# Cross attention from split halves, both token tiles in one values product, and seven weight buffers instead of nine

## The chip, the core and the metric

The kernel runs on one core of a Trainium2 chip. The core has five engines with a queue each: TensorE (PE in the profile, with its weight loads as PEld), VectorE (DVE), ScalarE (ACT), GpSimd (POOL) and SyncE (SP), which here issues the weight transfers. The metric is the device time of one execution in microseconds.

## What is computed

Two transformer blocks run over one sequence of 256 tokens with a model width of 1024. The first has four layers. Each layer is a mixer (sliding-window attention, a gated linear recurrence, latent attention, sliding-window attention again), then a cross attention over 256 memory tokens, then a convolutional gated feed-forward part with a hidden width of 2816; each of the three ends in a residual sum and a layer norm. The second block has a dilated attention beside a retention, an MLP and a per-layer embedding part. The change is in the cross attention and in what is shared by all:

```python
def memory_cross_attention(x, mem_k, mem_v, w_q, w_o):
    q = (x @ w_q).reshape(bsz, s, X_HEADS, X_HEAD_DIM)          # 4 heads of 256
    sc = jnp.einsum('bshd,bmhd->bhsm', q, mem_k) * (X_HEAD_DIM ** -0.5)
    p = jax.nn.softmax(sc, axis=-1)
    o = jnp.einsum('bhsm,bmhd->bshd', p, mem_v).reshape(bsz, s, D_MODEL)
    return o @ w_o

mem_k, mem_v = jnp.split(mem @ mem_w_kv, 2, axis=-1)            # once, for all four layers
```

All inputs and outputs are float32.

## The kernel before

The 256 tokens are two tiles of 128 (t = 0, 1). Most products are made of halves: `split` (L204 to L206) makes a high part with a ScalarE copy that rounds to the type fp32r, and a low part with a VectorE subtraction of it. A product is then three fp32r matmuls, high x high, high x low, low x high (`mm_nat` L219 to L221, weights as the moving side; `mm_T` L227 to L229, weights as the stationary side).

Weights stream from HBM. A tile is 128 x 1024 numbers, loaded by SP into one of five raw buffers and split in two halves of 512 columns into a `wh` and a `wl` buffer, of which there are nine each (L388, `self.wp`). ScalarE's copy into a buffer can start when TensorE has run the last matmul on the tile that had the buffer before, and VectorE's subtraction follows the copy. A projection of both token tiles with a width of 1024 goes over eight tiles: those of the first pass (t = 0) are used again in the pass over t = 1, so eight tiles are wanted at a time. Output projections do this in `out_steps` (L348 to L358), whose first token tile has the PSUM banks `acc, acc` and whose second has `po, tq`.

The order of instructions on each engine is not the order of the code: a scheduler places each instruction when it estimates that its inputs and a free buffer are there. So the number of buffers has a part in the order of all engines. At run time each engine runs its instructions in the placed order, one after another.

Names in the profile: `b0` to `b3` are the layers of the first block; `swa`, `lru`, `mla` the mixers, `mo` a mixer's output projection, `x` the cross attention, `xo` its output projection, `f` the feed-forward part. `dp0` is the first projection of the second block.

Cross attention (L457 to L524): the query of one token tile and half of the heads (`n`) is projected, copied to SBUF (L467), transposed by TensorE into the bank `tq` and copied by VectorE (L470); the scores are sixteen float32 matmuls of 256 columns (L480) per layer; the softmax follows (L483 to L492), the turn of the probabilities (transposes, one ScalarE copy L499), and the values as thirty-two float32 matmuls of 128 columns (L508), for one token tile and half at a time, from K and V of the memory that `memkv` made in the first mixer (L446, L453). A helper, `Skew`, issues the four units in a staggered order.

In the recurrent mixer of layer 1 (`b1lru`) the last gate needs TensorE's last matmul of the input projection, a `tanh` on ScalarE (L914, with a table load ahead of it) and a scan on VectorE (L904), and only then comes the last operand of the output projection `b1mo` (L924).

Of the kernel before, what the change touches and what calls it, by code (L numbers as in the profile page):

```python
# [19 lines left out]
P = 128  # L20
# [56 lines left out]
def col(n):  # L77
    return slice(n * 512, n * 512 + 512)


def tok(t):
    return slice(t * P, (t + 1) * P)
# [86 lines left out]
class Net:  # L169
# [117 lines left out]
    def T_split(self, src, hi, lo, n=4):  # L287
        self.split(self.transp(src, n), hi, lo)

    def rsqrt(self, v, n, eps):  # L290
# [136 lines left out]
    def memkv(self, mp):  # L427
# [3 lines left out]
        for t in range(NT):  # L431
# [6 lines left out]
        self.memk = self.memp.tile([P, KD, T], F32, name="memk")  # L438
        self.memv = self.memp.tile([P, 2, D], F32, name="memv")
# [17 lines left out]
    def cross(self, i):  # L457
# [3 lines left out]
        sc = 256.0 ** -0.5  # L461

        def query(t, n):
# [4 lines left out]
            pt = self.transp(q, 4, "tq")  # L468
            qT = self.s("q", [4, P])
            nc.vector.tensor_copy(qT, pt)  # L470
            return qT

        def attn(t, n, qT):
            p = self.s("p", [2, T])

            def scores():
                pss = self.ps("sc", (2, T))
                for h in range(2):
                    for k in range(2):
                        nc.tensor.matmul(pss[:, h], qT[:, 2 * h + k], self.memk[:, 4 * n + 2 * h + k],  # L480
                                         start=k == 0, stop=k == 1)
                nm = self.tiny("nm", [2])
                nc.vector.tensor_reduce(nm, pss, AX, ALU.max)  # L483
                nc.vector.tensor_scalar_mul(nm, nm, -sc)
                sm = self.tiny("den", [2])
                for h in range(2):
                    nc.scalar.activation(p[:, h], pss[:, h], AF.Exp, bias=nm[:, h : h + 1], scale=sc,
                                         accum_out=sm[:, h : h + 1])
                rs = self.tiny("rd", [2])
                nc.vector.reciprocal(rs, sm)  # L490
                for h in range(2):
                    nc.vector.tensor_scalar_mul(p[:, h], p[:, h], rs[:, h : h + 1])  # L492

            pTs = []

            def turn():
                pTs.append(self.s("pT", [2, 2, P]))
                pt = self.transp(p.rearrange("p a n -> p (a n)"))
                nc.scalar.activation(pTs[0].rearrange("p a b n -> p (a b) n"), pt, AF.Copy)  # L499

            def values():
                pT = pTs[0]
                po = self.ps("po", (4, P))
                for h in range(2):
                    for dt in range(2):
                        for m in range(2):
                            c = (2 * n + h) * 256 + dt * P
                            nc.tensor.matmul(po[:, 2 * h + dt], self.memv[:, m, c : c + P], pT[:, h, m],  # L508
                                             start=m == 0, stop=m == 1)
                sl = (slice(None), slice(4 * n, 4 * n + 4), tok(t))  # L510
                self.split(po, oTh[sl], oTl[sl])

            return scores, turn, values

        sk = Skew()
        todo = [(t, n) for t in range(NT) for n in range(2)]
        qs = [query(*todo[0])]
        for x, tn in enumerate(todo):
            if x + 1 < len(todo):
                qs.append(query(*todo[x + 1]))  # L520
            sk.unit(*attn(*tn, qs[x]))
        sk.flush()
        self.phase += "o"
        self.out_proj(self.cols(I["x_w_o"][i], 0, D), oTh, oTl, self.ln_tail(i, 1))  # L524


    def ffn_cols(self, i):
# [535 lines left out]
    def block1(self):  # L1063
        I = self.I
        n = 0
        with ExitStack() as c2:
# [9 lines left out]
            for i in range(DEPTH):  # L1076
# [18 lines left out]
                    return True  # L1095
                self.phase = f"b{i}x"
                cc = self.ffn_cols(i)
                self.cross(i)
                n += 1
                if n == self.stop:  # L1100
                    return True
# [588 lines left out]
```

## Time and profile before

| | us |
|---|---|
| median of 3 runs (2049.38 to 2052.22) | 2050.79 |
| the profiled execution | 2047.92 |
| its span | 2046.1 |
| TensorE busy | 2018.9 (99%), 10759 records |
| VectorE busy | 1586.5 (78%) |
| ScalarE busy | 1244.9 (61%) |
| HBM read over the span | 175 GB/s |

The profile is of one execution. The granted clock of TensorE is a share of full speed (1.0 is 2.4 GHz, 0.5 is 1.2 GHz). A float32 matmul leaves two records, an fp32r matmul one. The duration of a matmul in a row is longer than its place in the queue, since matmuls overlap: what one costs is read from the distance between the starts of neighbours.

### The profile page before, as it was taken

Reading aid. Unit: us, or ns where it says so; the run is one execution under the profiler, and the core shown is the slowest. Engines: PE = TensorE matmul, PEld = TensorE weight load, DVE = VectorE, ACT = ScalarE, POOL = GpSimd, SP = SyncE. Lnnn points to the kernel's source line nnn. Section 1 sums busy time; section 2 is a strip of 40 time slices with the busy share of each in tenths; the row PEclk is TensorE's granted clock in tenths of the full one; section 3 lists DMA queues with packets and bytes.
Section 4 is the critical chain, followed back from the end, with each engine's and each line's share of the span. In section 5 each row is a group of like instructions: output and inputs, shape, how many; then the busy total and the mean of one; then the engine's idle time right before and its main releaser. Section 6 shows DMA issues by size and latency. Waiting matters only on the chain.

```text
span 2046.1 us, 30433 instructions
## 1 busy us (share of the span) xinstructions
PE 2018.9 (99%) x10759; PEld 1701.3 (83%) x10759; DVE 1586.5 (78%) x3146; ACT 1244.9 (61%) x2592; POOL 40.2 (2%) x55
## 2 busy tenths in 40 slices
PE   9999999999999999999999999999999999999998
PEld 7878888887888888888887788888998888788887
DVE  7766898899699887679888778988677666676666
ACT  6745766595477646457766557665676444556554
POOL 0000000000000000000000000000000000000000
PEclk9999999999999999999999999999999999999999
DMA  8463666447457544565654445764545555566662
GB/s 265 136 193 118 204 215 196 150 132 240 141 179 227 173 150 144 176 205 165 207 166 154 146 135 198 227 192 118 170 150 191 163 181 191 165 205 206 192 192 76
DMA packets 236809, 359.65 MB, mean 176 GB/s; under 512 B 13936, under 2 KB 157424, under 8 KB 236656
## 3 DMA queue, kind: packets, MB, share of 16 engines
q1 hardware_dynamic: 236656, 357.71, 54.8%
q8 instruction: 84, 1.38, 0.3%
q14 instruction: 69, 0.57, 0.1%
HBM read 356.60 MB, written 1.05 MB: 175 GB/s over the span
## 4 chain that ended last, share of the span: by engine, by line
PE 51%; DVE 4%; ACT 2%; issue 1%; DMA 1%; POOL 0%; SPq 0%; DVEq 0%; POOLq 0%; ACTq 0%
PE b2f.sc L253 2%; PE b2f.tr L253 2%; PE b3f.sc L253 1%; PE b3f.tr L253 1%; PE mlp.sc L253 1%; PE mlp.tr L253 1%; PE mlp.acc L219 1%; PE mlp.acc L221 1%; PE mlp.acc L220 1%; PE b3f.acc L219 1%; PE b3f.acc L220 1%; PE b3f.acc L221 1%; PE b2f.acc L221 1%; PE b2f.sc L257 1%; PE b2f.acc L219 1%; PE b2f.acc L220 1%
## 5 line engine op out<-in xcount | busy, mean ns | idle before, releaser
L206 DVE TENSOR_TENSOR mlp.wl<-mlp.raw,mlp.wh 128x512 fp32r<-128x512 f32 x132 | 86.1, 687 | 41.2 <-ACT mlp.wh L205 40.1
L205 ACT ACTIVATE mlp.wh<-mlp.raw 128x512 fp32r<-128x512 f32 x132 | 75.7, 624 | 37.8 <-PE mlp.tq L221 20.8
L205 ACT ACTIVATE b1f.wh<-b1f.raw 128x512 fp32r<-128x512 f32 x132 | 76.3, 623 | 30.0 <-PE b1xo.tq L221 11.0
L205 ACT ACTIVATE b2f.wh<-b2f.raw 128x512 fp32r<-128x512 f32 x132 | 76.1, 622 | 28.9 <-PE b2xo.tq L221 11.0
L205 ACT ACTIVATE b0f.wh<-b0f.raw 128x512 fp32r<-128x512 f32 x132 | 76.2, 622 | 27.9 <-PE b0xo.tq L221 11.0
L205 ACT ACTIVATE b3f.wh<-b3f.raw 128x512 fp32r<-128x512 f32 x132 | 76.4, 622 | 26.7 <-PE b3xo.tq L221 9.8
L206 DVE TENSOR_TENSOR b2f.wl<-b2f.raw,b2f.wh 128x512 fp32r<-128x512 f32 x132 | 85.6, 683 | 4.6 <-ACT b2f.wh L205 4.3
L206 DVE TENSOR_TENSOR b0f.wl<-b0f.raw,b0f.wh 128x512 fp32r<-128x512 f32 x132 | 85.5, 683 | 4.7 <-ACT b0f.wh L205 4.5
L206 DVE TENSOR_TENSOR b1f.wl<-b1f.raw,b1f.wh 128x512 fp32r<-128x512 f32 x132 | 85.4, 683 | 4.7 <-ACT b1f.wh L205 4.5
L206 DVE TENSOR_TENSOR b3f.wl<-b3f.raw,b3f.wh 128x512 fp32r<-128x512 f32 x132 | 85.7, 684 | 4.3 <-ACT b3f.wh L205 4.1
L253 PE MATMUL b3f.sc<-b3xo.xT,b3f.wh 128*128 128x512 f32 x144 | 52.4, 398 | 1.0 <-DVE b3f.e L563 1.0
L253 PE MATMUL b1f.sc<-b1xo.xT,b1f.wh 128*128 128x512 f32 x144 | 52.4, 398 | 0.0
L253 PE MATMUL b0f.sc<-b0xo.xT,b0f.wh 128*128 128x512 f32 x144 | 52.4, 398 | 0.0
L253 PE MATMUL b2f.sc<-b2xo.xT,b2f.wh 128*128 128x512 f32 x144 | 52.3, 397 | 0.0
L253 PE MATMUL b0f.tr<-b0xo.xT,b0f.wh 128*128 128x512 f32 x144 | 51.7, 394 | 0.0
L253 PE MATMUL b1f.tr<-b1xo.xT,b1f.wh 128*128 128x512 f32 x144 | 51.7, 394 | 0.0
L253 PE MATMUL b3f.tr<-b3xo.xT,b3f.wh 128*128 128x512 f32 x144 | 51.7, 394 | 0.0
L253 PE MATMUL b2f.tr<-b2xo.xT,b2f.wh 128*128 128x512 f32 x144 | 51.7, 394 | 0.0
L563 DVE SCALAR_TENSOR_TENSOR b0f.e<-b0f.p,b0x.cols,b0f.e 128x255 f32<-128x255 f32 (+1 forms) x72 | 34.2, 479 | 7.0 <-ACT b0f.e L561 6.6
L563 DVE SCALAR_TENSOR_TENSOR b2f.e<-b2f.p,b2x.cols,b2f.e 128x255 f32<-128x255 f32 (+1 forms) x72 | 34.2, 479 | 6.6 <-ACT b2f.e L561 6.1
L563 DVE SCALAR_TENSOR_TENSOR b1f.e<-b1f.p,b1x.cols,b1f.e 128x255 f32<-128x255 f32 (+1 forms) x72 | 34.2, 478 | 6.5 <-ACT b1f.e L561 6.0
L563 DVE SCALAR_TENSOR_TENSOR b3f.e<-b3f.p,b3x.cols,b3f.e 128x255 f32<-128x255 f32 (+1 forms) x72 | 34.2, 479 | 5.6 <-ACT b3f.e L561 5.1
(1651 smaller groups left out, 7073.2 us busy)
## 6 DMA issues: line engine op xcount, KB each, us to landing
b0f.raw<-in_f_w_up_dram SPq DMA_DIRECT2D x44, 512.0 KB
b1f.raw<-in_f_w_up_dram SPq DMA_DIRECT2D x44, 512.0 KB
b2f.raw<-in_f_w_up_dram SPq DMA_DIRECT2D x44, 512.0 KB
b3f.raw<-in_f_w_up_dram SPq DMA_DIRECT2D x44, 512.0 KB
mlp.raw<-in_w_up_dram SPq DMA_DIRECT2D x32, 512.0 KB
mlp.raw<-in_w_down_dram SPq DMA_DIRECT2D x32, 512.0 KB
b0f.raw<-in_f_w_down_dram SPq DMA_DIRECT2D x22, 512.0 KB
b1f.raw<-in_f_w_down_dram SPq DMA_DIRECT2D x22, 512.0 KB
```

What stands on the lines that cost most here:

```text
L205: self.nc.scalar.activation(hi, src, AF.Copy)
L206: self.nc.vector.tensor_sub(lo, src, hi.bitcast(F32))
L219: mm(ps, Th[:, k, tok(t)], wh, start=start, stop=False)
L220: mm(ps, Th[:, k, tok(t)], wl, start=False, stop=False)
L221: mm(ps, Tl[:, k, tok(t)], wh, start=False, stop=stop)
L253: mm(ps.rearrange("p a n -> p (a n)"), wh[:, cs], self.xT[:, k].rearrange("p a n -> p (a n)"), start=k == 0, stop=k == w.K - 1)
L257: mm(ps[:, 1], wl[:, cs], self.xTh[:, k], start=False, stop=False)
L563: nc.vector.scalar_tensor_tensor(hc[:, j, s:], ps[j][:, : T - s], cc[:, 2 - s, f : f + 1], hc[:, j, s:], ALU.mult, ALU.add)
```

## The change

K and V of the memory are kept as high and low parts (two `split`s in place of the copies). The query's transposes are split as well. Scores and values become three fp32r matmuls each, in `mm3`. The values of one half of the heads are made for both token tiles at once, 256 columns wide, one bank per head: `po` and `tq` for the first half, two `sc` banks for the second. The steps are written out by hand: scores, turns and queries of the four units, the first values, six steps of the output projection, the last turn, two more steps, the second values, the rest. The output projection is made ahead of that, with its layer norm's two vectors. A pool of its own holds the high parts of the turned probabilities. The buffers of split weights, `wh` and `wl`, are seven each instead of nine, for the whole kernel.

```diff
-        self.wp = self.pool("w", 9)
+        self.wp = self.pool("w", 7)
@@ memkv
-                nc.scalar.activation(self.memk[:, 2 * p + j], ps, AF.Copy)
+                self.split(ps, *(a[:, 2 * p + j] for a in self.memk))
...
-                nc.scalar.activation(self.memv[:, t, col(n)], ps, AF.Copy)
+                self.split(ps, *(a[:, t, col(n)] for a in self.memv))
@@ cross
+    def mm3(self, ps, a, b, start, stop):
+        (ah, al), (bh, bl) = a, b
+        mm = self.nc.tensor.matmul
+        mm(ps, ah, bh, start=start, stop=False)
+        mm(ps, ah, bl, start=False, stop=False)
+        mm(ps, al, bh, start=False, stop=stop)
...
-            qT = self.s("q", [4, P])
-            nc.vector.tensor_copy(qT, pt)
+            qT[t, n] = [self.s("q", [4, P], F32R) for _ in range(2)]
+            self.T_split_tq(q, *qT[t, n])
...
-                        nc.tensor.matmul(pss[:, h], qT[:, 2 * h + k], self.memk[:, 4 * n + 2 * h + k],
-                                         start=k == 0, stop=k == 1)
+                    self.mm3(pss[:, h], [a[:, 2 * h + k] for a in qT[t, n]],
+                             [a[:, 4 * n + 2 * h + k] for a in self.memk], k == 0, k == 1)
...
-                nc.scalar.activation(pTs[0].rearrange("p a b n -> p (a b) n"), pt, AF.Copy)
+            for h in range(2):
+                self.split(pt[:, 2 * h : 2 * h + 2], *(a[:, :, tok(t)] for a in pTs[n][h]))
...
-                            nc.tensor.matmul(po[:, 2 * h + dt], self.memv[:, m, c : c + P], pT[:, h, m],
-                                             start=m == 0, stop=m == 1)
+                po = self.ps(tags[h], (2, T))
+                        self.mm3(po[:, dt], [a[:, m, c : c + P] for a in self.memv],
+                                 [a[:, m] for a in pTs[n][h]], m == 0, m == 1)
...
-        sk = Skew()
-        todo = [(t, n) for t in range(NT) for n in range(2)]
...
+        query(0, 0)
+        query(0, 1)
+        scores(0, 0)
+        query(1, 0)
+        turn(0, 0)
+        scores(0, 1)
+        scores(1, 0)
+        query(1, 1)
+        turn(0, 1)
+        turn(1, 0)
+        scores(1, 1)
+        values(0, ("po", "tq"))
+        some(6)
+        turn(1, 1)
+        some(2)
+        values(1, ("sc", "sc"))
+        for _ in out:
+            pass
```

The order of the instructions moves in many places. Two of them are shown. The first is the end of the recurrent mixer of layer 1. On ScalarE before, two whole tiles (four halves) of the output projection's weights, `b1mo.wh`, are copied among the gates, well ahead of the tail:

```order
L205 ACTIVATE b1mo.wh_4815<-b1mo.raw_4813 128x512
L889 ACTIVATE b1lru.p_4529<-b1lru.p_4529,b1lru.c_734_4042 128x256
L205 ACTIVATE b1mo.wh_4815<-b1mo.raw_4813 128x512
L205 ACTIVATE b1mo.wh_4829<-b1mo.raw_4827 128x512 x2
L898 ACT_TABLE_LOAD
L898 ACTIVATE b1lru.b_4377<-b1lru.b_4377 128x1024
```

In the changed kernel the last tiles of the mixer's own input projection, `b1lru.wh`, stand in that place:

```order
L205 ACTIVATE b1lru.wh_4816<-b1lru.raw_4814 128x512
L205 ACTIVATE b1lru.wh_4836<-b1lru.raw_4834 128x512 x2
L920 ACT_TABLE_LOAD
L920 ACTIVATE b1lru.b_4467<-b1lru.b_4467 128x1024
L934 ACTIVATE b1lru.e_4697<-b1lru.acc_4632 128x512
```

and the first copies of `b1mo.wh` come behind the last `tanh`, which is the last of these rows ahead of them:

```order
L920 ACT_TABLE_LOAD
L920 ACTIVATE b1lru.b_4710<-b1lru.b_4710 128x1024
L936 ACT_TABLE_LOAD
L936 ACTIVATE b1lru.e_4878<-b1lru.e_4878 128x512
L205 ACTIVATE b1mo.wh_4905<-b1mo.raw_4903 128x512 x2
L205 ACTIVATE b1mo.wh_4919<-b1mo.raw_4917 128x512 x2
L205 ACTIVATE b1lru.oTh_4805<-b1lru.e_4697 128x512
```

So four halves have moved behind the tail's ScalarE work. On VectorE, correspondingly, the first subtraction for the output projection stands behind the tail's last two operations (L946 here, L924 before):

```order
L926 SCALAR_TENSOR_TENSOR b1lru.u_4142<-b1lru.g_4709,b1lru.b_4710 128x256
L946 SCALAR_TENSOR_TENSOR b1lru.e_4697<-b1lru.e_4697,b1lru.u_4142 128x512
L946 SCALAR_TENSOR_TENSOR b1lru.e_4878<-b1lru.e_4878,b1lru.u_4142 128x512
L206 TENSOR_TENSOR b1mo.wl_4906<-b1mo.raw_4903,b1mo.wh_4905 128x512
L206 TENSOR_TENSOR b1lru.oTl_4806<-b1lru.e_4697,b1lru.oTh_4805 128x512
L206 TENSOR_TENSOR b1mo.wl_4906<-b1mo.raw_4903,b1mo.wh_4905 128x512
L206 TENSOR_TENSOR b1lru.oTl_4806<-b1lru.e_4878,b1lru.oTh_4805 128x512
```

Before, the four halves of the first two tiles stood 15 to 26 rows earlier; here none does. TensorE's rows at that place begin, before, with both parts of the first tile,

```order
L219 MATMUL b1mo.acc_4811<-b1mo.wh_4815,b1lru.oTh_4715 128x512
L220 MATMUL b1mo.acc_4811<-b1mo.wl_4816,b1lru.oTh_4715 128x512
L219 MATMUL b1mo.acc_4812<-b1mo.wh_4815,b1lru.oTh_4715 128x512
L220 MATMUL b1mo.acc_4812<-b1mo.wl_4816,b1lru.oTh_4715 128x512
L221 MATMUL b1mo.acc_4811<-b1mo.wh_4815,b1lru.oTl_4716 128x512
L221 MATMUL b1mo.acc_4812<-b1mo.wh_4815,b1lru.oTl_4716 128x512
```

and, in the changed kernel, with all four uses of the first tile's high part, for which no low part is needed:

```order
L219 MATMUL b1mo.acc_4901<-b1mo.wh_4905,b1lru.oTh_4805 128x512
L219 MATMUL b1mo.acc_4902<-b1mo.wh_4905,b1lru.oTh_4805 128x512
L219 MATMUL b1mo.po_5031<-b1mo.wh_4905,b1lru.oTh_4805 128x512
L219 MATMUL b1mo.tq_5032<-b1mo.wh_4905,b1lru.oTh_4805 128x512
L220 MATMUL b1mo.acc_4901<-b1mo.wl_4906,b1lru.oTh_4805 128x512
L221 MATMUL b1mo.acc_4901<-b1mo.wh_4905,b1lru.oTl_4806 128x512
```

The second place is an output projection (`b1xo`) on TensorE. Before, the second token tile's pass (`po`, `tq`) begins when all eight weight tiles have been used for the first:

```order
L219 MATMUL b1xo.acc_5389<-b1xo.wh_5487,b1x.oTh_5032 128x512
L220 MATMUL b1xo.acc_5389<-b1xo.wl_5488,b1x.oTh_5032 128x512
L221 MATMUL b1xo.acc_5389<-b1xo.wh_5487,b1x.oTl_5033 128x512
L219 MATMUL b1xo.po_5518<-b1xo.wh_5392,b1x.oTh_5032 128x512
L220 MATMUL b1xo.po_5518<-b1xo.wl_5393,b1x.oTh_5032 128x512
L221 MATMUL b1xo.po_5518<-b1xo.wh_5392,b1x.oTl_5033 128x512
L219 MATMUL b1xo.tq_5519<-b1xo.wh_5392,b1x.oTh_5032 128x512
L220 MATMUL b1xo.tq_5519<-b1xo.wl_5393,b1x.oTh_5032 128x512
L221 MATMUL b1xo.tq_5519<-b1xo.wh_5392,b1x.oTl_5033 128x512
```

In the changed kernel the eighth tile (`wh_5652`) is used in the middle of the second pass, four matmuls behind the last use of the first tile (`wh_5518`), whose buffer it takes:

```order
L221 MATMUL b1xo.tq_5684<-b1xo.wh_5518,b1x.oTl_5126 128x512
L219 MATMUL b1xo.po_5683<-b1xo.wh_5532,b1x.oTh_5125 128x512
L220 MATMUL b1xo.po_5683<-b1xo.wl_5533,b1x.oTh_5125 128x512
L221 MATMUL b1xo.po_5683<-b1xo.wh_5532,b1x.oTl_5126 128x512
L219 MATMUL b1xo.tq_5684<-b1xo.wh_5532,b1x.oTh_5125 128x512
L219 MATMUL b1xo.acc_5514<-b1xo.wh_5652,b1x.oTh_5125 128x512
L220 MATMUL b1xo.tq_5684<-b1xo.wl_5533,b1x.oTh_5125 128x512
L219 MATMUL b1xo.acc_5515<-b1xo.wh_5652,b1x.oTh_5125 128x512
L220 MATMUL b1xo.acc_5514<-b1xo.wl_5653,b1x.oTh_5125 128x512
L221 MATMUL b1xo.acc_5514<-b1xo.wh_5652,b1x.oTl_5126 128x512
```

The same pattern, four matmuls between the last use of the first tile and the first use of the eighth, stands at 26 places of the changed kernel: in the query, mixer, feed-forward and output projections of the four layers and in the second block.

## Rows read from the trace of the kernel before

**Rows 1.** Page, the span and the busy time of the engines.

```profile
span 2046.1 us, 30433 instructions
...
PE 2018.9 (99%) x10759; PEld 1701.3 (83%) x10759; DVE 1586.5 (78%) x3146; ACT 1244.9 (61%) x2592; POOL 40.2 (2%) x55
```

**Rows 2.** Waits of TensorE: engine, tile, line, releaser: total us, times, longest us.

```profile
PE b1mo.acc L219 <- ACT b1mo.wh L205: 1.9, 1, 1.9
...
PE b2mla.po L221 <- DVE b1f.xT L206: 1.1, 1, 1.1
...
PE dp0.tr L284 <- DVE b3f.pT L1131: 1.0, 1, 1.0
```

**Rows 3.** Timeline of TensorE, cross attention of layer 1: start us, us, operation.

```profile
502.45 1.02 PE L480 MATMUL b1x.sc<-memk,b1x.q 128*128 128x256 f32 x4
503.31 0.64 PE L284 MATMUL b1x.tq<-ident,b1x.e 128*128 128x128 f32 x4
...
512.77 1.95 PE L508 MATMUL b1x.po<-b1x.pT,memv 128*128 128x128 f32 x16
514.55 0.49 PE L284 MATMUL b1x.tr<-ident,b1x.p 128*128 128x128 f32 x3
```

**Rows 4.** Timeline of TensorE, products of 256 columns, layer 1.

```profile
417.54 0.28 PE L227 MATMUL b1lru.acc<-b0f.xT,b1lru.wh 128*128 128x256 f32 x1
...
418.38 0.28 PE L228 MATMUL b1lru.acc<-b0f.xT,b1lru.wh 128*128 128x256 f32 x1
```

**Rows 5.** Timeline of ScalarE and VectorE, copies and subtractions of 512 and 256 columns.

```profile
505.29 0.60 ACT L499 ACTIVATE b1x.pT<-b1x.tr 128x512 f32<-128x512 f32 x1 [1.01 <-PE b1x.tr L284]
...
1411.19 0.42 DVE L206 TENSOR_TENSOR dp0.wl<-dp0.raw,dp0.wh 128x256 fp32r<-128x256 f32 x1
```

**Rows 6.** Lines, K of the memory: duration ns least/median/most, first and last start.

```profile
L446 ACT ACTIVATE memk<-b0swa.acc x8: 359/368/401, 68.4 to 92.2; 128x256 f32<-128x256 f32 x8
```

**Rows 7.** Windows, cross attention of layer 1: us, then busy us (x) of PE, PEld, DVE, ACT.

```profile
480.30:526.20 45.90, 45.01 (x249) 37.19 (x249) 35.46 (x70) 23.56 (x52) 0.92 (x1) 1.00 0.58 195
```

**Rows 8.** Timeline of TensorE, end of the recurrent mixer of layer 1.

```profile
450.92 0.28 PE L229 MATMUL b1lru.tq<-b0f.xT,b1lru.wl 128*128 128x256 f32 x1
451.91 0.50 PE L219 MATMUL b1mo.acc<-b1mo.wh,b1lru.oTh 128*128 128x512 f32 x1 [0.71 <-ACT b1lru.oTh L205]
...
455.98 0.40 PE L221 MATMUL b1mo.po<-b1mo.wh,b1lru.oTl 128*128 128x512 f32 x1
458.24 0.50 PE L219 MATMUL b1mo.acc<-b1mo.wh,b1lru.oTh 128*128 128x512 f32 x1 [1.86 <-ACT b1mo.wh L205]
...
461.58 0.63 PE L221 MATMUL b1mo.tq<-b1mo.wh,b1lru.oTl 128*128 128x512 f32 x1
```

**Rows 9.** Timeline of ScalarE and VectorE, the same stretch.

```profile
436.80 0.62 ACT L205 ACTIVATE b1mo.wh<-b1mo.raw 128x512 fp32r<-128x512 f32 x1
...
437.81 1.67 ACT L205 ACTIVATE b1mo.wh<-b1mo.raw 128x512 fp32r<-128x512 f32 x3
...
457.04 0.63 ACT L914 ACTIVATE b1lru.e<-b1lru.e 128x512 f32<-128x512 f32 x1
457.57 2.17 ACT L205 ACTIVATE b1mo.wh<-b1mo.raw 128x512 fp32r<-128x512 f32 x4
...
459.91 1.27 DVE L924 SCALAR_TENSOR_TENSOR b1lru.e<-b1lru.e,b1lru.u 128x512 f32<-128x512 f32 x2
461.10 0.68 DVE L206 TENSOR_TENSOR b1mo.wl<-b1mo.raw,b1mo.wh 128x512 fp32r<-128x512 f32 x1
```

**Rows 10.** Windows, after the recurrent mixer: PEclk is the third figure from the end.

```profile
461.00:463.00 2.00, 2.00 (x6) 1.54 (x6) 2.00 (x5) 2.00 (x5) 0.52 (x1) 0.50 0.82 252
464.00:466.00 2.00, 2.00 (x10) 1.64 (x9) 2.00 (x5) 0.89 (x2) 0.00 (x0) 1.00 0.91 225
```

**Rows 11.** Timeline of TensorE and ScalarE, a weight tile freed and its successor copied.

```profile
544.66 0.40 PE L221 MATMUL b1xo.tq<-b1xo.wh,b1x.oTl 128*128 128x512 f32 x1
...
545.14 0.63 ACT L205 ACTIVATE b1f.wh<-b1f.raw 128x512 fp32r<-128x512 f32 x1 [1.54 <-PE b1xo.tq L221]
```

More of the change, by code (lines that the diff above doesn't have):

```diff
@@ L288, in T_split, with T_split_tq @@
         self.split(self.transp(src, n), hi, lo)
+    def T_split_tq(self, src, hi, lo):
+        self.split(self.transp(src, 4, "tq"), hi, lo)
     def rsqrt(self, v, n, eps):
@@ L437, in memkv @@
             yield
-        self.memk = self.memp.tile([P, KD, T], F32, name="memk")
-        self.memv = self.memp.tile([P, 2, D], F32, name="memv")
+        self.memk = [self.memp.tile([P, KD, T], F32R, name=n) for n in ("memkh", "memkl")]
+        self.memv = [self.memp.tile([P, 2, D], F32R, name=n) for n in ("memvh", "memvl")]
         W = I["mem_w_kv"]
@@ L452, in memkv, with cross @@
                 self.proj_nat(ps, *mT, t, w)
-                nc.scalar.activation(self.memv[:, t, col(n)], ps, AF.Copy)
+                self.split(ps, *(a[:, t, col(n)] for a in self.memv))
                 yield
-    def cross(self, i):
+    def mm3(self, ps, a, b, start, stop):
[4 more added lines that the diff above has]
+        mm(ps, al, bh, start=False, stop=stop)
+    def cross(self, i, pool):
         nc, I = self.nc, self.I
@@ L461, in cross @@
         sc = 256.0 ** -0.5
+        qT, p = {}, {}
+        pTs = [[(pool.tile([P, 2, T], F32R, name=self.nm("pTh")), self.s("pT", [2, T], F32R)) for _ in range(2)]
+               for _ in range(2)]
         def query(t, n):
@@ new lines, in scores @@
+        def scores(t, n):
+            p[t, n] = pr = self.s("p", [2, T])
+            pss = self.ps("sc", (2, T))
+            for h in range(2):
+                for k in range(2):
+                    self.mm3(pss[:, h], [a[:, 2 * h + k] for a in qT[t, n]],
+                             [a[:, 4 * n + 2 * h + k] for a in self.memk], k == 0, k == 1)
+            nm = self.tiny("nm", [2])
+            nc.vector.tensor_reduce(nm, pss, AX, ALU.max)
+            nc.vector.tensor_scalar_mul(nm, nm, -sc)
+            sm = self.tiny("den", [2])
+            for h in range(2):
+                nc.scalar.activation(pr[:, h], pss[:, h], AF.Exp, bias=nm[:, h : h + 1], scale=sc,
+                                     accum_out=sm[:, h : h + 1])
+            rs = self.tiny("rd", [2])
+            nc.vector.reciprocal(rs, sm)
+            for h in range(2):
+                nc.vector.tensor_scalar_mul(pr[:, h], pr[:, h], rs[:, h : h + 1])
@@ new lines, in turn, with values @@
+        def turn(t, n):
+            pt = self.transp(p[t, n].rearrange("p a n -> p (a n)"))
+            for h in range(2):
+                self.split(pt[:, 2 * h : 2 * h + 2], *(a[:, :, tok(t)] for a in pTs[n][h]))
+        def values(n, tags):
+            for h in range(2):
+                po = self.ps(tags[h], (2, T))
+                for dt in range(2):
+                    c = (2 * n + h) * 256 + dt * P
+                    for m in range(2):
+                        self.mm3(po[:, dt], [a[:, m, c : c + P] for a in self.memv],
+                                 [a[:, m] for a in pTs[n][h]], m == 0, m == 1)
+                f = slice(4 * n + 2 * h, 4 * n + 2 * h + 2)
+                self.split(po, oTh[:, f], oTl[:, f])
@@ new lines, in cross, with some @@
+        out = self.named(self.phase + "o", self.out_steps(self.cols(I["x_w_o"][i], 0, D), oTh, oTl, self.ln_tail(i, 1)))
+        def some(n):
+            for _ in islice(out, n):
+                pass
[13 more added lines that the diff above has]
+        turn(1, 1)
@@ L527, in ffn_cols @@
+        some(2)
+        values(1, ("sc", "sc"))
+        for _ in out:
+            pass
     def ffn_cols(self, i):
@@ L1097, in block1 @@
                 cc = self.ffn_cols(i)
-                self.cross(i)
+                with self.tc.tile_pool(name=f"x{i}", bufs=1) as xpool:
+                    self.cross(i, xpool)
                 n += 1
```

41 lines of the change are left out of this document (removed).

## The prediction

> **What bounds the kernel now.** First the page: TensorE is busy for 2018.9 of the 2046.1 us of the span, 99% [rows 1]. It leaves 27 us, part of which are the start and the end. So the time falls only if TensorE has less work, and rises with every microsecond that it waits. Second, its waits: the longest is 1.9 us, for a weight copy behind the recurrent mixer of layer 1 (`b1mo`); two others of 1.1 and 1.0 us stand in the latent attention and at the start of the second block [rows 2]. VectorE and ScalarE have slack on the whole (78 and 61%). Third, the timeline at the places that the change touches: one cross attention and the end of the recurrent mixer. The terms below are made against the profiled execution, 2047.92 us, which is 2.87 us under the median of 2050.79; I add the net change to the median.
>
> **Scores and values.** Two float32 score matmuls of 256 columns take from 502.45 to 503.31, where the next operation starts: 0.43 us each, and 16 of them 6.9 us. Eight float32 value matmuls of 128 columns take from 512.77 to 514.55: 0.222 each, and 32 of them 7.1 us [rows 3]. Together 14.0 us in a cross attention. The changed kernel has 48 + 48 = 96 fp32r matmuls, all of 256 columns, each with a new stationary tile. The same kind stands in the recurrent mixer: seven steps from 417.54 to 418.38, 0.12 us each [rows 4]. 96 x 0.12 = 11.5. That is 2.5 us less in a cross attention and **10.0 us** less in the four. Projection, transposes and output projection are as before. TensorE is busy for 45.01 of the 45.90 us of one cross attention [rows 7], so all of this is on the path.
>
> **Copies and subtractions around them.** In each cross attention the query's turned halves need four ScalarE copies more (0.60 each, by the copy of 512 columns [rows 5]), and VectorE's copies become subtractions of the same width. The turn of the probabilities has two ScalarE copies of 256 columns for one of 512 (2 x 0.37 [rows 6] for 0.60), and two VectorE subtractions that are new (0.42 each by the row of 256 columns [rows 5]). So ScalarE gets 4 x 0.60 + 4 x 0.14 = 3.0 us and VectorE 8 x 0.42 = 3.4 us more in 45.9 us, in which they are busy for 23.6 and 35.5 [rows 7]. ScalarE has room. VectorE comes to 39 us in some 43; it does not bound the sum, but it may be late at a turn. From the turn to the values the path is one subtraction longer, 0.42; in the new order six or more matmuls stand between (some 1.4 us). I take 0 for it; at worst each of the four cross attentions loses a subtraction at two places, 4 x 2 x 0.42 = 3.4 us. The memory's K and V get twelve new subtractions in the first mixer (8 x 0.42 + 4 x 0.68 = 6.1 us of VectorE), beside TensorE work that does not wait for them before the first scores, 50 us later: 0. The two layer-norm vectors are loaded earlier by SP, ahead of weights that are wanted later still: 0. Without that cover a weight tile would come later by the time of one vector's load, below 2 us.
>
> **Seven buffers: the recurrent mixer.** Before, two tiles of `b1mo` are split ahead of the mixer's tail (four ScalarE halves from 436.80 on [rows 9]), so TensorE works while the tail runs on the other two engines: 18 matmuls from 451.91 to 455.98, then 1.86 us of waiting until 458.24, and nine more until 461.58 [rows 8]. 27 matmuls are started by 461.8. In the new order the first copy of `b1mo` stands behind the `tanh` of 457.04 to 457.57, where the third tile's stands now, so its first half is there at about 458.2; the four uses of this tile's high part take until 459.2. Its first low half stands behind the two operations of 459.91 on VectorE, and is there at 461.10 + 0.68 = 461.8 [rows 9]. So four matmuls are started by then and not 27. The distance of two such matmuls is (455.98 - 451.91) / 17 = 0.24, counting from the first, and 0.233 in the steady part; 23 x 0.233 = **5.4 us lost**. Nothing gives it back: after 461.8 TensorE has no wait in this projection now. If ScalarE and VectorE reach the tail earlier without the four splits, the tail starts at most as much earlier as VectorE's one half in the last stretch lasts (0.68), bound below by TensorE's last gate product at 450.92. Lower bound of the loss: 4. After the waits the granted clock is 0.50 in 461 to 463, 1.2 GHz, and 1.00 again from 464 [rows 10]: the row of 461.58 has 0.63 where that of 455.98 has 0.40. About 3 us at half rate cost 1.5 us today. The new wait is longer, and if the low clock lasts twice as long, another 1.5 is lost. Upper bound: 7.
>
> The Trainium skill, TensorE: Matmul & The Clock Gate, section "What's actually happening", says that the array's clock is throttled by default and that work releases it, with the two levels 1.2 and 2.4 GHz and none between. The trace agrees (0.50 in 461 to 463 [rows 10]). By this rule the second start, at 461.8 in place of 458.24, begins at the low level as well, and the sum would be some 1.5 us higher than with the clock left out; by the row, a low stretch as long as the present one, it is unchanged.
>
> **Seven buffers: the eighth tile.** At 26 places the eighth tile gets the buffer of the first, and four matmuls (4 x 0.233 = 0.93 us) stand between the last use of the one and the first use of the other. That last use lasts 0.40 from its start; a copy that waits for such a release starts 0.08 after it (544.66 + 0.40 = 545.06, and 545.14) and takes 0.63 [rows 11]. From the start of the last use: 0.40 + 0.08 + 0.63 = 1.11 until the high half is there; TensorE wants it 5 x 0.233 = 1.17 after the same start. The low half takes 0.68 more, 1.8, and is wanted three matmuls later, at 1.87. So each place just fits if ScalarE and VectorE are free at that moment, and loses what they are still busy with otherwise: between 0 and one operation (0.68). Over 26 places the bounds are 0 and 17.7 us. The order has the split next on both engines at the places that I read, so I take 0.12 a place, near the lower end: **3 us lost**. The other tiles keep a lead of several microseconds.
>
> **Seven buffers: waits that move.** In the latent attention the wait of 1.1 us [rows 2] goes away, since the subtraction that it waits for now stands ahead of other work; the norms of both token tiles then come late together, and I expect as much waiting there: 0, with bounds -1.4 and +3. At `dp0` a layer norm's four operations now stand ahead of the splits of the fourth to sixth tile, beside the 1.0 us wait that is there now: +1, with bounds -1 and +3.
>
> **Sum.** -10.0 + 5.4 + 3 + 1 = -0.6 us, so 2050.2 us. The bounds add up to -10.0 + 4 + 0 - 2.4 = -8.4 and -10.0 + 7 + 17.7 + 6 + 3.4 = +24; the latter needs each place at its worst, so the range is cut at +10.
>
> **Rivals.** (a) The forecast: TensorE's saving is used up by the two losses. 0.42.
>
> (b) The saving stays. Speaking for it: two splits fit at nearly every one of the 26 places, and the tail loses its lower bound. -10.0 + 4 + 1 - 1 = -6, so 2044.8 us. Against it: ScalarE and VectorE are busy for 61 and 78% of the time, so a split often finds something ahead. 0.33.
>
> (c) Slower: TensorE starves at the eighth tile. VectorE, busy at 78%, has an operation of 0.68 running or queued at most of the 26 places; half of one is 0.34, times 26 = 8.8, and the sum -10.0 + 5.4 + 8.8 + 1 = +5.2, 2056 us. The time is above the 0.2% from 0.30 us a place on. For it: the reserve is 0.06 us by the rows. Against it: the order was placed with that wait in view. 0.19.
>
> (d) The cross attention is not paced by TensorE any more: with 39 of 43 us VectorE is late at the turns and the splits, and of the 10.0 us only half shows. -5 + 5.4 + 3 + 1 = +4.4, 2055.2 us. The window of layer 1 speaks for it, the other layers have less VectorE work. 0.06.
>
> **How the numbers follow.** A measurement of this kernel tells a change of about 0.2%, 4.1 us, from none: faster is below 2046.7, slower above 2054.9. (a) spreads by some 4 us about 2050.2, so part of it falls on either side: faster 0.33, same 0.42, slower 0.25. The range of 2041 to 2060 has (b) with room for a tail that costs less, and (c) to +9.
>
> **What would show it.** Scores and values: starts of 0.12 us and about 11.5 us for all of a layer's; 0.13 or more would cost 1 us a layer. The mixer: one wait of 6 to 7 us at `b1mo` for the copy and one of 2 to 3 for the subtraction, with a low clock after it; if `b1mo` begins before the `tanh`, that term is wrong. The eighth tile: waits below 0.3 us at some of the 26 places by `wh` or `wl`; more than 0.3 at most of them is (c). TensorE's busy time falls by about 10 us. I am wrong if its idle time grows by less than 5 or more than 15 us.

## The result and the profile after

The changed kernel takes 2068.88 us (median of 4 runs, 2068.4 to 2070.84) where the kernel before takes 2050.70 beside it: slower by 18 us, a ratio of 1.0088 with an interval of 1.0076 to 1.0099. The forecast was 2050.2, its range 2041 to 2060; the time lies outside. The two profiled executions stand 21.1 us apart by their spans, because that of the kernel before lies 2.8 us under its median; the differences below are of these two.

The page after, where [rows 1] stand for before:

```profile
span 2067.2 us, 30525 instructions
...
PE 2027.2 (98%) x10759; PEld 1694.0 (82%) x10759; DVE 1600.5 (77%) x3190; ACT 1255.3 (61%) x2624; POOL 39.4 (2%) x55
```

TensorE's busy time was to fall by 10 us and rose by 8; its idle time grew by 13. The waits of TensorE after (engine, tile, line, releaser: total us, times, longest), against [rows 2]:

```profile
PE b1mo.acc L219 <- ACT b1mo.wh L205: 5.5, 1, 5.5
PE mlp.acc L219 <- ACT mlp.q L205: 1.8, 1, 1.8
PE dp0.acc L220 <- DVE dp0.wl L206: 1.5, 1, 1.5
PE b1mo.acc L220 <- DVE b1mo.wl L206: 1.4, 1, 1.4
...
PE b1lru.tq L229 <- DVE b1lru.wl L206: 1.3, 1, 1.3
...
PE b0x.sc L464 <- ACT b0x.q L205: 0.6, 1, 0.6
...
PE b0f.tr L284 <- DVE x L330: 0.2, 1, 0.2
```

The one at `b1mo` was forecast. Those of `mlp`, `dp0`, `b1lru`, and the small ones of `b?x.sc` and `b?f.tr` (one in each layer) were not, or not so large. But TensorE's idle time grew by only 13 of the 21 us, so the waits don't say where all of the time went. What does is the time from a phase's first matmul to the next phase's, read from both traces:

| phases | before, us | after, us | difference |
|---|---|---|---|
| four cross attentions with output projection | 261.4 | 258.3 | -3.1 |
| four feed-forward parts | 744.2 | 750.6 | +6.4 |
| recurrent mixer of layer 1 with output projection | 89.1 | 95.8 | +6.7 |
| the three other mixers | 314.4 | 316.6 | +2.2 |
| dilated projections and attention | 172.3 | 175.3 | +3.0 |
| retention, gate, output projections | 245.2 | 245.5 | +0.3 |
| MLP | 187.0 | 190.5 | +3.5 |
| per-layer embedding | 23.6 | 25.1 | +1.5 |

The cross attention gives 3 us and not 10, the recurrent mixer costs about what was forecast (5.4), and the rest, forecast at 4, costs 17. One execution was profiled of each kernel: the first mixer alone spreads from 138.2 to 142.2 us over the runs below, so the row of the three other mixers is uncertain by about as much as it shows.

**The recurrent mixer.** TensorE's timeline after, answering to [rows 8]:

```profile
450.88 0.39 PE L229 MATMUL b1lru.tq<-b0f.xT,b1lru.wl 128*128 128x256 f32 x1 [1.33 <-DVE b1lru.wl L206]
...
460.01 1.32 PE L219 MATMUL b1mo.acc<-b1mo.wh,b1lru.oTh 128*128 128x512 f32 x2 [5.52 <-ACT b1mo.wh L205]
...
461.56 0.63 PE L219 MATMUL b1mo.tq<-b1mo.wh,b1lru.oTh 128*128 128x512 f32 x1
463.61 0.79 PE L220 MATMUL b1mo.acc<-b1mo.wl,b1lru.oTh 128*128 128x512 f32 x1 [1.43 <-DVE b1mo.wl L206]
```

After the mixer's last input product come two waits, 5.5 and 1.4 us, and only four matmuls between them. ScalarE and VectorE there, answering to [rows 9]:

```profile
458.81 0.63 ACT L936 ACTIVATE b1lru.e<-b1lru.e 128x512 f32<-128x512 f32 x1
459.35 1.13 ACT L205 ACTIVATE b1mo.wh<-b1mo.raw 128x512 fp32r<-128x512 f32 x2
```

```profile
461.69 1.26 DVE L946 SCALAR_TENSOR_TENSOR b1lru.e<-b1lru.e,b1lru.u 128x512 f32<-128x512 f32 x2
462.88 0.68 DVE L206 TENSOR_TENSOR b1mo.wl<-b1mo.raw,b1mo.wh 128x512 fp32r<-128x512 f32 x1
```

The first copy of `b1mo` starts behind the `tanh`, the first subtraction behind L946, as the order said. The granted clock, answering to [rows 10] (third figure from the end):

```profile
460.00:465.00 5.00, 3.56 (x7) 2.24 (x8) 5.00 (x10) 4.14 (x8) 0.00 (x0) 0.50 0.41 93
465.00:470.00 5.00, 5.00 (x15) 3.88 (x14) 5.00 (x9) 1.91 (x5) 0.00 (x0) 0.59 0.94 324
...
468.00:469.00 1.00, 1.00 (x4) 0.76 (x3) 1.00 (x3) 0.00 (x0) 0.00 (x0) 0.50 0.82 188
469.00:470.00 1.00, 1.00 (x6) 0.82 (x5) 1.00 (x2) 0.25 (x1) 0.00 (x0) 0.96 0.96 328
```

It is 0.50 (1.2 GHz) over the whole of 460 to 465 and, by windows of one microsecond, up to 469; before, it was low for some three microseconds (0.50 from 461 to 463, 0.65 in the window on either side). So the low clock lasts nearly three times as long under TensorE's matmuls as before, where the forecast's upper bound had taken twice as long.

**The cross attention.** TensorE after, at the end of the first layer's (answers to [rows 3]):

```profile
171.51 0.93 PE L284 MATMUL b0x.tr<-ident,b0x.p 128*128 128x128 f32 x7
172.36 0.66 PE L284 MATMUL b0x.tq<-ident,b0x.e 128*128 128x128 f32 x4
172.86 0.27 PE L284 MATMUL b0x.tr<-ident,b0x.p 128*128 128x128 f32 x1
173.77 0.39 PE L464 MATMUL b0x.sc<-memkh,b0x.q 128*128 128x256 f32 x1 [0.64 <-ACT b0x.q L205]
173.99 0.28 PE L465 MATMUL b0x.sc<-memkl,b0x.q 128*128 128x256 f32 x1
174.32 0.38 PE L464 MATMUL b0x.po<-b0x.pTh,memvh 128*128 128x256 f32 x1
174.58 0.39 PE L466 MATMUL b0x.sc<-memkh,b0x.q 128*128 128x256 f32 x1
174.80 0.28 PE L464 MATMUL b0x.sc<-memkh,b0x.q 128*128 128x256 f32 x1
```

The last scores start after a wait of 0.64 us, for the query's high half; the two products that need only this half run, then the low half is late as well (174.58 for 174.11 at 0.12 us a step, with one product of the values between), and from 174.80 on the products follow at 0.12 us. ScalarE in the same stretch:

```profile
171.71 0.60 ACT L483 ACTIVATE b0x.e<-b0x.acc 128x512 f32<-128x512 f32 x1
172.20 0.38 ACT L205 ACTIVATE b0x.pTh<-b0x.tr 128x256 fp32r<-128x256 f32 x1
172.47 0.63 ACT L205 ACTIVATE b0xo.wh<-b0xo.raw 128x512 fp32r<-128x512 f32 x1
173.12 0.60 ACT L205 ACTIVATE b0x.q<-b0x.tq 128x512 fp32r<-128x512 f32 x1
```

The query's copy (L483) ends at 172.3, its transposes end at about 173.0; ScalarE meanwhile copies a turned half and half a weight tile, and turns to the query at 173.12. By then TensorE has no matmul of the projection left. Taken over the trace from start to start, scores are 6.5 to 6.6 us in each layer after (6.3 to 7.9 before) and values 5.9 to 6.2 (7.1): 50.1 us in the four layers for 56.1, which is 6.1 less. About half of that is lost again: the last transpose ahead of the last scores is followed by the next product after 0.91 us (172.86 to 173.77), where one transpose of a pack follows another after 0.11. That is 0.8 us a layer, of which 0.64 appears as a wait.

### The profile page after: what moved, and what is told of

Its sections match the earlier page's. It is cut to its first block, busy times and chain, and to the rows that moved or that the text cites. A ratio compares the mean times of both kernels' runs of the same rounds, so it can differ in the third digit from the quotient of the medians.

```text
span 2067.2 us, 30525 instructions
## 1 busy us (share of the span) xinstructions
PE 2027.2 (98%) x10759; PEld 1694.0 (82%) x10759; DVE 1600.5 (77%) x3190; ACT 1255.3 (61%) x2624; POOL 39.4 (2%) x55
## 4 chain that ended last, share of the span: by engine, by line
PE 85%; DVE 9%; ACT 3%; issue 2%; DMA 1%; POOL 0%; DVEq 0%; POOLq 0%; ACTq 0%
PE b1f.sc L253 2%; PE b0f.sc L253 2%; PE b2f.sc L253 2%; PE b1f.tr L253 2%; PE b0f.tr L253 2%; PE b2f.tr L253 2%; PE b3f.sc L253 1%; PE b3f.tr L253 1%; PE mlp.sc L253 1%; PE mlp.tr L253 1%; PE mlp.acc L219 1%; PE mlp.acc L220 1%; PE mlp.acc L221 1%; PE b2f.sc L257 1%; PE b0f.sc L257 1%
## 5 line engine op out<-in xcount | busy, mean ns | idle before, releaser
L257 PE MATMUL b2f.sc<-b2xo.xT,b2f.wl 128*128 128x256 f32 x144 | 37.5, 281 | 0.0
```

What stands on the lines that cost most here:

```text
L257: mm(ps[:, 1], wl[:, cs], self.xTh[:, k], start=False, stop=False)
```

## The experiments

All were timed in three rounds beside the kernel before on the same chip; its median was 2050.2 to 2051.4 in them. "Phase" times are read as in the table above.

**Seven buffers alone, and eight.** In the kernel before:

```diff
-        self.wp = self.pool("w", 9)
+        self.wp = self.pool("w", 7)      # the other run: 8
```

> The kernel before with seven buffers of split weights in place of nine and nothing else. Theory A (the seven buffers cost the time, everywhere where a layer norm or a mixer's tail was covered by matmuls on tiles split ahead; the new cross attention itself saves 3 us): about +21 us, 2070 to 2073. Rival B (the new order of the cross attention, with the output projection made ahead, costs the time; the buffers cost only what was forecast, 9 us with the tail of the recurrent mixer): 2056 to 2061.

> The kernel before with eight buffers in place of nine. Theory A in the form that eight live tiles are the point (seven is one too few for a pass over eight tiles): +0 to +4 us, 2050 to 2055. Rival (each buffer is worth the same cover): half of the cost of two, about +10, 2060. Theory B: 2052 to 2056.

Seven: 2076.14 us, ratio 1.0126 (1.0111 to 1.0141), +25.9. Eight: 2053.09, ratio 1.0014 (1.0005 to 1.0023), +2.8. Theory B falls: the buffers by themselves cost more than the whole change does. They cost even more than theory A had said (2070 to 2073), so the cross attention gives not 3 but 7 to 8 us at equal buffers (2076.1 to 2068.9, or 25.9 less 18.2 against the kernel before). The traces of the two kernels agree with that: the cross attentions take 6.4 us less in the changed kernel, and no other row of the table differs by more than 0.3. And the eighth buffer is worth 23 us, the ninth 3. The phases show what each buys: with seven, the feed-forward parts take 750.7 us, with eight 744.3, as with nine (744.2); the cross attentions take 264.6, 259.6 and 261.4. The recurrent mixer takes 95.9, 92.7 and 89.1 and the MLP 190.5, 188.5 and 187.0, so these two still lose with eight; the three other mixers take 316.5, 317.0 and 314.4.

How a feed-forward part loses is seen at the second token tile's transposes. TensorE before (first layer):

```profile
212.85 0.60 PE L284 MATMUL b0f.tr<-ident,x 128*128 128x128 f32 x4
...
215.37 0.60 PE L284 MATMUL b0f.tr<-ident,x 128*128 128x128 f32 x4
```

with eight buffers:

```profile
214.10 0.60 PE L284 MATMUL b0f.tr<-ident,x 128*128 128x128 f32 x4
...
216.62 0.60 PE L284 MATMUL b0f.tr<-ident,x 128*128 128x128 f32 x4
```

with seven, and VectorE ahead of it:

```profile
211.87 0.39 PE L219 MATMUL b0f.acc<-b0f.wh,b0xo.xT 128*128 128x512 f32 x1
212.53 1.29 PE L284 MATMUL b0f.tr<-ident,x 128*128 128x128 f32 x8 [0.28 <-DVE x L327]
213.85 0.50 PE L219 MATMUL b0f.acc<-b0f.wh,b0xo.xT 128*128 128x512 f32 x1
```

```profile
210.32 1.40 DVE L326 SCALAR_TENSOR_TENSOR x<-x,b0xo.mv,b0xo.vec 128x512 f32<-128x512 f32 x2
211.65 1.40 DVE L327 SCALAR_TENSOR_TENSOR x<-x,b0xo.rs,b0xo.vec 128x512 f32<-128x512 f32 x2
212.97 2.49 DVE L206 TENSOR_TENSOR b0f.wl<-b0f.raw,b0f.wh 128x512 fp32r<-128x512 f32 x4
```

The low parts that VectorE makes ahead of that norm, before (eight halves in a row) and with seven:

```profile
197.92 4.90 DVE L206 TENSOR_TENSOR b0f.wl<-b0f.raw,b0f.wh 128x512 fp32r<-128x512 f32 x8
```

```profile
202.93 1.28 DVE L206 TENSOR_TENSOR b0f.wl<-b0f.raw,b0f.wh 128x512 fp32r<-128x512 f32 x2
```

The part begins with the first token tile's products on eight weight tiles, three for each half of a tile. When the second token tile's norm starts on VectorE (L326), the low parts of 14 halves are made with nine buffers, of 12 with eight and of 8 with seven. With eight or nine, 33 products stand ahead of the second tile's transposes, which come in two packs, and the norm is long done by then (211.58 before). With seven, the 8 halves last for 24 products; the 25th (211.87) needs a high part alone, and the low part that comes next is made behind the norm, from 212.97 on. In the placed order TensorE turns to the second tile here, whose norm ends at 213.05. From the 25th product to the first transpose it takes 0.66 us in place of 0.23; the second four transposes follow the first four after 0.31 and not 0.11, behind the norm's second half; the next product follows after 0.30, for ScalarE's copy of what was turned, where it was 0.03 before. That makes 0.9 of the 1.2 us that this phase loses, and only 0.28 of it appears as a wait. All four layers have the 25 products, the pack of eight and the wait of 0.28 with seven.

The half that is missing is the first of the fifth tile, not of the eighth. That it is what brought the transposes forward in the order is read from these rows and was not tried by itself. The eighth tile's first use comes 13.7 us after the start of the phase, where two steps take 0.31 and 0.27 us for 0.23: 0.13 us.

**A shorter layer norm, with seven and with nine.** The scale by the deviation and the shift are left out of the norms of the first block whose result is transposed:

```diff
-            nc.vector.scalar_tensor_tensor(xn, xn, rstd, b[:, col(n)], ALU.mult, ALU.add)
+            if not xT:
+                nc.vector.scalar_tensor_tensor(xn, xn, rstd, b[:, col(n)], ALU.mult, ALU.add)
```

> The kernel before with seven buffers, and every layer norm of the first block whose result is transposed leaves out its last two VectorE operations (the scale by the deviation and the shift, 1.33 us of VectorE a token tile), so the output is another. Theory L (with seven tiles TensorE has run all of the first token tile's work, less the eighth tile, before the second tile's layer norm is done; the wait for that norm is what the feed-forward phases lose): the feed-forward phases lose at most 0.4 us each and not 1.2 to 2.8, and the gap to the same kernel with nine buffers shrinks by 4 to 6 us, from 26 to 20 to 22. Rival (the eighth tile's own copy and subtraction are late, whatever the norm): the gap stays within 2 us of 26.

> The same shortened layer norm in the kernel before with its nine buffers, for the run beside it (the last two VectorE operations of each such layer norm are left out). No norm is waited for there but at 0.6 and 0.9 us places, so 0 to 3 us less than the kernel before, 2047.5 to 2050.5.

Seven: 2069.95 us. Nine: 2049.80 (ratio to the kernel before 0.9994, 0.9985 to 1.0004). The gap is 20.2 us, within theory L's 20 to 22 and not the rival's 26. The feed-forward parts of the first three layers lose 0.2, 0.3 and 0.2 us (the fourth 1.6), and the transposes stand in packs of four again:

```profile
215.38 0.60 PE L284 MATMUL b0f.tr<-ident,x 128*128 128x128 f32 x4
```

So the norm's VectorE time is what seven buffers leave uncovered at these places, and it accounts for 5.7 us of the 25.9. Theory L's words are not borne out, though: with seven TensorE had run 25 of the first token tile's products and not all of seven tiles' (42). The run by itself doesn't part two forms: the transposes wait for the norm, and weight subtractions queue behind it on VectorE; both get 1.33 us earlier. In the trace with seven both are there. Of the 20.2 us that remain, by the phases of the two kernels with the shorter norm, 6.0 are the recurrent mixer's, 3.2 stand in the feed-forward parts and cross attentions, 3.0 in the three other mixers and 7.5 in the second block, whose norms the run leaves as they are. What costs the time in these last two was not tried.

**Nine buffers in the recurrent mixer alone**, seven elsewhere:

```diff
+            turn = net.turn = getattr(net, "turn", 0) + 1
+            if own is not None and turn % 9 > 6:      # own: a pool of two pairs, open in layer 1's mixer
+                h, l = (own.tile([P, 1024], F32R, tag=x, name=net.nm(x)) for x in ("wh", "wl"))
```

> The kernel before with seven buffers, but nine while the recurrent mixer of layer 1 and its output projection run (two more pairs from a pool of their own, for two of every nine tiles). Theory: the mixer's loss (95.9 us for mixer and output projection with seven, 89.1 with nine) is only the split-ahead tiles of its output projection and the clock after the wait; it goes back to 89 to 91, the wait of 5.5 us at b1mo to about 2, and the kernel from 2076 to 2069 to 2071. Rival (what is late there comes from the phases ahead, or from the raw buffers): the mixer keeps 94 us or more, and the kernel 2074 or more.

2071.35 us, 4.8 less than with seven throughout, and 0.35 above the 2069 to 2071 of the theory. The mixer with its projection takes 90.4 us (95.9, and 89.1 with nine throughout). The wait of 5.5 us with seven and, with eight, of

```profile
PE b1mo.acc L219 <- ACT b1mo.wh L205: 4.0, 1, 4.0
```

is back at its length of [rows 2]:

```profile
PE b1mo.acc L224 <- ACT b1mo.wh L210: 1.9, 1, 1.9
```

Most of the mixer's loss is its own two buffers, as forecast: 5.5 of 6.7 us.

**Scores alone and values alone**, with eight buffers, which is what fits once either K or V is kept twice:

```diff
 # scores: K and the query in halves, values as before
-                        nc.tensor.matmul(pss[:, h], qT[:, 2 * h + k], self.memk[:, 4 * n + 2 * h + k],
+                        self.mm3(pss[:, h], [a[:, 2 * h + k] for a in qT],
+                                 [a[:, 4 * n + 2 * h + k] for a in self.memk], k == 0, k == 1)
 # values: the changed kernel with K, query and scores of before
```

> The kernel before with K of the memory and the query in halves and the scores as three products; values, their order and the turn as before; eight buffers. Scores took 6.5 us of TensorE after and 6.7 before, so theory A says within 2 us of the kernel before with eight buffers. The forecast's size (16 x 0.43 to 48 x 0.12 = 5.8, 1.1 us a layer) would give 4 us less than that kernel.

> The changed kernel's values, turn and order, with float32 K, query and scores as before, and eight buffers. Values took 5.9 to 6.15 us after and 7.1 before: theory A says 3 to 5 us less than the kernel before with eight buffers, and no wait of 0.64 us at the last scores for the query's high half if that wait comes from the second copy. Theory B (the order itself costs): slower than the kernel before with eight buffers.

Scores: 2050.28 us; values: 2050.64. Both are even with the kernel before (ratios 1.0001 and 1.0002) and 2.8 and 2.5 us below it with eight buffers. For the scores, theory A said within 2 us and the forecast's size 4: it lies between. For the values, theory A's 3 to 5 was too much, and the wait at the last scores is there without split halves too, for VectorE's plain copy:

```profile
PE b0x.sc L493 <- DVE b0x.q L486: 0.7, 1, 0.7
```

So the new order brings that wait without the second copy.

**The wait at the last scores.** Two moves, on the changed kernel with seven buffers, and on the values alone with eight:

```diff
 # a_ord                                        # a_q6_r4 and v_w8_q
-        scores(1, 1)                           -        scores(1, 0)
         values(0, ("po", "tq"))                         query(1, 1)
+        scores(1, 1)                           +        scores(1, 0)
-        some(6)                                # a_q6_r4 as well: six query buffers, four raw
+        some(8)
         turn(1, 1)
-        some(2)
```

> The changed kernel (seven buffers) with the first values ahead of the last scores, and eight output-projection steps ahead of the last turn. Theory: the wait of 0.64 us a layer at the last scores is for the query's split halves with nothing left to run, and the 24 matmuls of the first values (2.9 us) cover it: 2.6 us less than the changed kernel, 2066.3, if the last turn does not get late in its place. Rival (the chain from the last scores to the last turn, softmax and splits, is what needs the cover): the wait moves to the last turn or the second values, 2069 or more.

> The changed kernel (seven buffers) with six query buffers instead of four, the last query ahead of the third scores, and four raw buffers instead of five to make room. Theory: the last query is late because its two halves wait for buffers; made a step earlier, its splits lie beside the third scores, and the wait of 0.64 us a layer goes: 2066 to 2067. Rival: it is late because TensorE has no other work there, whatever the buffers: unchanged within 1 us, 2068 to 2070.

> Float32 scores, the values of both token tiles as three fp32r products, eight buffers, and the last query ahead of the third scores. The wait of 0.7 to 0.9 us a layer at the last scores is for the last query's transposes and copy. If that query is just late in the order: 2 to 3 us less than the same kernel without the move (2050.6), 2047.6 to 2048.6, which would be under the kernel before. If TensorE has nothing left to run at that point whichever comes first: the wait moves to the turn, 2050 to 2052.

`a_ord`: 2067.58 us, 1.3 less than the changed kernel (ratio to before 1.0083, 1.0068 to 1.0098; the intervals overlap). The wait did not move:

```profile
PE b0x.sc L464 <- ACT b0x.q L205: 0.6, 1, 0.6
```

The first values need the turn that is released in the same microsecond, so no values stand ahead of the scores; this run tells nothing on the cover. `v_w8_q`: 2063.50 us, 12.9 more than without the move. The wait moved to the turn and doubled, 1.4 us in place of 0.7:

```profile
PE b0x.tr L284 <- DVE b0x.p L505: 1.4, 1, 1.4
```

Behind it comes another of 0.59 us, for the copy of what was turned, and then the clock falls (the third figure from the end):

```profile
178.00:180.00 2.00, 2.00 (x11) 2.00 (x11) 0.32 (x1) 0.60 (x1) 0.00 (x0) 0.50 0.00 0
```

The values there stand 0.21 us apart in place of 0.12. The four cross attentions take 12.2 us more than without the move. The softmax of the third scores now starts a query later. Theory "late in the order" falls. The other one had the turn right as the place, but the time is 11.5 us above its 2050 to 2052: it had neither the second wait nor the clock. The chain at the end of a cross attention has no TensorE work beside it, and these moves only put it at another place. `a_q6_r4`: 2094.21 us, outside both of its ranges, with a wait of 1.6 us at the turn as well; but four raw buffers come with the move, and with three raw buffers the kernel before takes 55 us more (below), so the time can't be read for the order.

**Raw buffers.** To fit eight split buffers into the changed kernel, three raw buffers; the same in the kernel before; and the reverse trade there, eight split and seven raw:

```diff
-        self.raw = self.pool("raw", 5)
+        self.raw = self.pool("raw", 3)        # a_w8_r3 (split 8), b_w9_r3 (split 9); b_w8_r7: 7 (split 8)
```

> The changed kernel with eight buffers of split weights and, to make room, three raw buffers instead of five. Theory A (eight live tiles need eight buffers): the loss of the seven goes, all but the recurrent mixer's, and the cross attention's gain stays: 2053.1 less 1.3 to 1.8 us in each of four layers, 2045.5 to 2048. Rival: the new order of the cross attention needs the cover of nine buffers as well, or three raw buffers starve the splits: above 2051.

> The kernel before with three raw buffers instead of five, for the side effect of the run beside it. If the raw buffers carry no cover (the splits wait for split buffers and not for the load): within 2 us of 2050.3. If they do, several us more, and the run beside it is to be read against that.

> The kernel before with eight buffers of split weights and, in the room of the ninth pair, seven raw buffers instead of five. Three raw buffers cost 55 us, so raw buffers carry the cover of the loads. If five still leave some of it open, 2046 to 2050, below the kernel with eight and five (2053.1); if five hold all of it, 2052 to 2054, and the ninth split buffer is the better use of the room.

2097.05, 2105.73 and 2051.82 us. Three raw buffers cost the kernel before 55 us, since ScalarE's copies now wait for loads; its waits for the fourth layer's weights with three,

```profile
ACT b3f.wh L205 <- DMA b3f.raw<-in_f_w_up_dram: 23.2, 23, 3.7
```

and with five:

```profile
ACT b3f.wh L205 <- DMA b3f.raw<-in_f_w_up_dram: 6.7, 7, 3.0
```

With both at three raw buffers the changed kernel with eight is 8.7 us faster than the kernel before with nine, and its cross attentions take 12.6 us less. Its gain is there, but there is no room to have it: the rival of that run is right for the time, and theory A's number was not reached. Seven raw buffers with eight split are even with the kernel before (ratio 1.0001, 0.9992 to 1.0011), which lies between the two answers that were expected. No kernel that was run beats the kernel before beyond its interval.

## Why the prediction was wrong

**Scores and values** (-10.0): wrong in size. By starts they take 6.1 us less, and at equal buffers the kernel gains 7 to 8. The step of 0.12 us holds (173.99 and 174.80 on), but the term counted every product at this step, 11.5 us a layer where 12.4 to 12.7 were measured. And "I take 0 for it", of the path around the turns, had no wait where the new order leaves TensorE without work: at the last scores it is 0.8 us a layer by starts, 3.2 in all, near the bound of 3.4. That bound was for late subtractions; the run of the values alone has the wait with a query that is not split, so it is near by luck.

**Copies in the first mixer, earlier vectors** (0): they don't show; the other three mixers lose 2.0 us with seven buffers alone and 2.2 with the whole change.

**The recurrent mixer** (5.4, bounds 4 to 7): right. 6.7 us, and 5.5 of them come back with two buffers there. The first copy of `b1mo` starts 66.6 us after the mixer's first matmul, where the forecast's 457.6 gives 66.4. The waits were 5.5 and 1.4 us, forecast 6 to 7 and 2 to 3. The wait of 1.3 us for the mixer's own last subtraction was not foreseen; it adds nothing, since TensorE would have stood still later (1.3 and 5.5 are 6.8). The low clock after them lasted longer than forecast. Some 5.4 us of matmuls at half rate behind the second wait cost 2.7 by estimate, for 1.5 before, and the difference is about what 6.7 has over 5.4.

**The eighth tile** (3, bounds 0 to 17.7): the step that failed. It asked only whether the eighth tile's copy and subtraction come in time after their buffer is free. There they cost about what was taken: 0.13 us at the place in the first feed-forward part, for 0.12. An estimate from the trace with seven, the steps between TensorE's starts that end on a split part of any tile outside the recurrent mixer, is 5 us more than with nine, most of it in the second block. The sentence that failed is "The other tiles keep a lead of several microseconds". In the feed-forward part the low part of the fifth tile was there 3.2 us ahead of the phase's first product before; with seven it comes behind a layer norm on VectorE, 7.2 us after that product, when TensorE has wanted it for 1.6 us. What stands next in TensorE's order are the transposes of that norm's result, so it waits for the norm. Outside the recurrent mixer the phases lose 20.5 us with seven buffers (27.3 over all phases, less 6.7) and 2 with eight. The forecast had 4 for them. With a shorter norm 6.8 of the 20.5 go by the phases, so the norm's VectorE time is shown for a third of it. For the rest, most of it in the second block and the other mixers, it is shown that the eighth buffer decides, but not by which wait; that stays open.

**Waits that move** (+1 at `dp0`, 0 in the latent attention): the dilated part lost 3.0 us, the upper bound for `dp0`. The latent attention lost 1.4, within its bounds. The MLP lost 3.5, and the forecast had no term for it; the wait of 1.8 us at `mlp` comes with eight buffers as well. Why it appears there was not tried.

**The signs.** TensorE's busy time was to fall by 10 us and rose by 8: that one told. Its idle time grew by 13, within the 5 to 15 that were to mean a right forecast. That was luck: the losses of the forecast come to 9.4 us, the kernel lost more than twice that, and only part of it counts as idle, since the record of one matmul (0.39 us in the feed-forward part) reaches over the start of the next (0.23).

**Rivals.** (c), starvation at the eighth tile, had the side right, and a VectorE that is busy with something else when a split is due; the place and the length were others, and its 2056 us was too low. (d) had the size of the cross attention's gain nearer (5 for 6.1 by starts), but for VectorE's load and not, as it was, for a chain without other work beside it.

## What to carry to other kernels

Count how many tiles a pass keeps alive before a buffer count is cut: here, for passes over eight tiles, the ninth buffer was worth 3 us and the eighth 23. With too few, the splits of all later tiles lose their lead, and some fall behind a long operation on the engine that makes them (here a layer norm), just where TensorE counted on them to cover that operation. In an engine that is 99% busy such a loss hardly appears as idle time; compare the traces phase by phase, from first matmul to first matmul. And test a resource that is cut to make room by itself, ahead of the change that it pays for.

## Not expected of the hardware

The granted clock stayed at 0.50 for nine microseconds after matmuls had started again at 460.0, with a second wait of 1.4 us among them; before, after waits of 1.9 and 0.6 us, it was back at 1.00 by 464. In the run with the query moved, waits of 1.44 and 0.59 us with four transposes between were followed by 0.50 from 178 to 180 us; in the changed kernel, with its one wait of 0.64 us there, it stayed at 1.00.
